# A fused LayerNorm and GELU: five-row buffers in four slots, with loads and stores on one queue

## The chip, the cores and the metric

One core of a Trainium2 chip. The time is that of one execution on the device, in microseconds (us), and lower is better. "Landing" means that one DMA engine has finished its share of a transfer and counted up the semaphore. A transfer is spread over 16 DMA engines, each with its own share of the rows, and it has landed when all 16 have counted.

## The reference

```python
x: (8, 1024, 2048) float32; gamma, beta: (2048,)
mean = np.mean(x, axis=-1, keepdims=True)
var = np.var(x, axis=-1, keepdims=True)
out = gamma * (x - mean) / np.sqrt(var + eps) + beta
return 0.5 * out * (1 + np.tanh(np.sqrt(2 / np.pi) * (out + 0.044715 * out ** 3)))
```

8192 rows of 8 KB are read once and written once: 67.1 MB in, 67.1 MB out.

## The kernel before

A buffer holds four rows for each of 128 partitions (4 MB), so a partition's share is one run of 32 KB. There are five slots and 16 buffers. SyncE issues the loads, ScalarE the stores; each has its own DMA queue. The result overwrites the input in its slot, so a slot is loaded again only when its store has landed.

```python
R = 4; SLOTS = 5; SPLIT = 3
...
@block.sync                                   # loads
for b in range(B):
    s = slot(b)
    if stored(b):
        sy.wait_ge(s_store[s], stored(b))     # the slot's last store has landed
    for q in range(R):
        if b == 0:       # four transfers of one row each
            sy.dma_start(out=xts[s][:, q:q + 1], in_=xg[0, :, q:q + 1]).then_inc(s_first[q], 16)
        elif b == SPLIT: # buffer 3 too
            sy.dma_start(out=xts[s][:, q:q + 1], in_=xg[b, :, q:q + 1]).then_inc(s_load[s], 16)
    if b not in (0, SPLIT):
        sy.dma_start(out=xts[s], in_=xg[b]).then_inc(s_load[s], 16 * R)
...
@block.vector                                 # k runs over the rows of all slots
    stats(s, q, (s_load[s], 16 * R) if q == 0 else None, k + 1)   # row t
    scale((q - 1) % R, k + 1)                                      # row t - 1
...
@block.scalar
for t in range(T + 1):
    if t < T:            # normalize row t
        ac.activation(out=yks[t % 2], in_=xts[slot(b)][:, q], func=ACT.Identity, ...)
    i = t - 1            # GELU of row t - 1, from PSUM into its slot
    ins = ac.activation(out=xt[:, q], in_=pss[i % 2], func=ACT.Gelu_apprx_tanh)._wait_ge(s_t, i + 1)
    if by_row(b):        # last buffer: a store per row
        ...
    elif q == R - 1:     # a store per buffer
        ins.then_inc(s_r, 1)
        ac.dma_start(out=og[b], in_=xt)._wait_ge(s_r, b + 1).then_inc(s_store[slot(b)], 16)
```

GpSimd computes the inverse deviation and the offset of a row, VectorE the statistics and the product with gamma, TensorE adds beta in PSUM. Mind the order on VectorE and ScalarE: the last row of a buffer is finished after the first row of the next buffer has been begun.

## Time and profile before

| | before |
|---|---|
| time | 320.19 us median (320.01 to 320.34, 4 runs) |
| span of the profiled run | 318.5 us |
| VectorE, ScalarE, TensorE busy | 78%, 79%, 77% |
| DMA, share of 16 engines | 98.4% |
| last load landed, all 16 engines | 285.0 us |

The page gives the rate in 40 equal slices and the DMA issues. The columns of an issue line are count, size, and time from issue to landing:

```profile
GB/s 289 438 457 401 394 434 430 444 424 436 432 424 444 417 453 416 440 440 416 457 403 457 420 436 444 411 461 403 453 432 424 449 407 457 424 432 403 453 396 209
...
out_dram<-xt ACTq DMA_DIRECT2D x15, 4096.0 KB, 32.6
```

Apart from the first slice (289), slice 5 (394) and the last (209) are the low ones. A store of 4 MB takes 32.6 us to land, over three times what its packets need alone (8 of 1.21 us on each engine, 9.7 us), because it shares the engines with the loads. The rest of the reading is in the prediction.

### The profile page before, as it was taken

The numbers are of one execution on the slowest core, as the hardware profiler recorded it, in microseconds if no ns is written. First come the engines' busy times: TensorE is split into PE (matmuls) and PEld (weight loads), VectorE is DVE, ScalarE is ACT, GpSimd is POOL, SyncE is SP. The second block draws the span as 40 slices with busy tenths as digits, with TensorE's granted clock in tenths as the row PEclk, the third lists the DMA queues.
The fourth block names the chain that finished last, engine by engine and source line by source line (L and its number), as shares of the span: only waits on it lengthen the run. The fifth ranks groups of instructions, "written<-read, shape, count | busy, mean of one in ns | idle before, by whom it ended". The sixth has DMA issues, their size and how long they took to land.

```text
span 318.5 us, 2090 instructions
## 1 busy us (share of the span) xinstructions
PE 244.3 (77%) x520; PEld 57.2 (18%) x520; DVE 247.5 (78%) x386; ACT 251.7 (79%) x132; POOL 110.6 (35%) x201
## 2 busy tenths in 40 slices
PE   2769999999999989687795868958589595886860
PEld 1212222222212112111121112212112121111110
DVE  3499999999999897786968968599686986869810
ACT  2769999999999989698696967969589695995970
POOL 1144444444444444232443333333332433324300
DMA  7999999999999999999999999999999999999995
GB/s 289 438 457 401 394 434 430 444 424 436 432 424 444 417 453 416 440 440 416 457 403 457 420 436 444 411 461 403 453 432 424 449 407 457 424 432 403 453 396 209
DMA packets 6002, 134.26 MB, mean 421 GB/s; under 512 B 704, under 2 KB 752, under 8 KB 752
## 3 DMA queue, kind: packets, MB, share of 16 engines
q1 hardware_dynamic: 3168, 67.11, 49.4%
q10 hardware_dynamic: 2832, 67.13, 49.0%
q14 instruction: 2, 0.02, 0.0%
HBM read 67.13 MB, written 67.11 MB: 421 GB/s over the span
## 4 chain that ended last, share of the span: by engine, by line
DMA 64%; ACT 14%; DVE 10%; POOL 5%; PE 3%; issue 1%; ACTq 0%; DVEq 0%; POOLq 0%; SPq 0%
DMA xt<-in_x_dram 32%; DMA out_dram<-xt 30%; ACT yk L195 9%; DVE sts L149 7%; ACT xt L202 4%; POOL ves L135 3%; DVE zg L158 2%; PE ps L220 2%; DMA rows<-in_gamma_dram 2%; POOL rss L137 2%; POOL nms L139 1%; DVE mvs L155 1%; PE ps L237 1%; ACT g_t L191 1%; ACTq L205 0%
## 5 line engine op out<-in xcount | busy, mean ns | idle before, releaser
L149 DVE BATCH_NORM_STATS2 sts<-xt 128x6 f32<-128x512 f32 x256 | 157.7, 679 | 33.5 <-DMA xt<-in_x_dram 31.9
L195 ACT ACTIVATE yk<-xt,nms,rss 128x2048 bf16<-128x2048 f32 x64 | 133.7, 2090 | 48.9 <-POOL nms L139 42.9
L237 PE MATMUL ps<-zg,ident 128*128 128x512 bf16 x256 | 120.8, 627 | 55.8 <-DVE zg L158 54.7
L233 PE MATMUL ps<-b_hl,ones_b 33*128 33x512 bf16 x256 | 120.6, 624 | 2.2 <-PEq L228 2.2
L202 ACT ACTIVATE xt<-ps 128x2048 f32<-128x2048 f32 x64 | 118.9, 1858 | 1.5 <-PE ps L237 1.5
L135 POOL TENSOR_SCALAR ves<-mvs 128x1 f32<-128x1 f32 x64 | 38.5, 602 | 179.2 <-DVE mvs L155 179.2
L158 DVE TENSOR_TENSOR zg<-yk,g_t 128x2048 bf16<-128x2048 bf16 x64 | 76.5, 1195 | 19.2 <-ACT yk L195 19.2
L237 PEld LDWEIGHTS ps<-zg,ident 128*128 128x128 bf16 x256 | 27.6, 130 | 149.0 <-DVE zg L158 113.7
L233 PEld LDWEIGHTS ps<-b_hl,ones_b 33*128 33x128 bf16 x256 | 27.0, 127 | 92.1 <-issue 88.4
L139 POOL TENSOR_SCALAR nms<-mvs,rss 128x1 f32<-128x1 f32 x64 | 35.7, 558 | 6.3
L137 POOL TENSOR_TENSOR rss<-ves,mhalf 128x1 f32<-128x1 f32 x64 | 35.3, 552 | 5.3
L155 DVE BATCH_NORM_AGGREGATE mvs<-sts 128x2 f32<-128x24 f32 x64 | 16.9, 264 | 2.2
L220 PE MATMUL ps<-rows,ones 1*128 1x512 f32 x8 | 7.2, 1076 | 6.1 <-DMA rows<-in_gamma_dram 6.1
L188 ACT ACTIVATE b_hl<-rows 1x2048 bf16<-1x2048 f32 x1 | 1.9, 1909 | 5.3 <-DMA rows<-in_beta_dram 5.3
L166 DVE TENSOR_TENSOR b_hl<-rows,b_hl 1x2048 bf16<-1x2048 f32 x1 | 2.3, 2280 | 2.8 <-ACT b_hl L189 2.8
L220 PEld LDWEIGHTS ps<-rows,ones 1*128 1x128 f32 x8 | 2.5, 327 | 9.2 <-DMA rows<-in_gamma_dram 6.1
L191 ACT ACTIVATE g_t<-ps 128x2048 bf16<-128x2048 f32 x1 | 1.9, 1877 | 1.9 <-PE ps L220 1.9
L184 ACT ACT_TABLE_LOAD x1 | 1.3, 1283 | 0.9 <-SPq L107 0.9
L189 ACT ACTIVATE b_hl<-rows 1x2048 bf16<-1x2048 f32 x1 | 1.9, 1908 | 0.0
L161 DVE MEMSET b_hl<- 33x1024 uint32 x1 | 0.9, 912 | 1.2 <-SPq L107 1.2
L126 POOL MEMSET ones<- 65x128 f32 x1 | 0.2, 202 | 0.5 <-SPq L107 0.5
L130 POOL TENSOR_SCALAR_AFFINE_SELECT ident<-ident 128x128 bf16<-128x128 bf16 x1 | 0.3, 295 | 0.1
(7 smaller groups left out, 0.9 us busy)
## 6 DMA issues: line engine op xcount, KB each, us to landing
out_dram<-xt ACTq DMA_DIRECT2D x15, 4096.0 KB, 32.6
xt<-in_x_dram SPq DMA_DIRECT2D x14, 4096.0 KB
xt<-in_x_dram SPq DMA_DIRECT2D x8, 1024.0 KB, 8.4
out_dram<-xt ACTq DMA_DIRECT2D x4, 1024.0 KB, 8.6
rows<-in_beta_dram ACTq DMA_DIRECT2D x2, 8.0 KB, 5.9
rows<-in_gamma_dram ACTq DMA_DIRECT2D x1, 8.0 KB, 5.1
```

The lines of the kernel that those rows point to most:

```text
L135: po.tensor_scalar(out=ves[:, c], in0=mvs[:, k, 1:2], scalar1=float(eps), scalar2=1.0, op0=ALU.add, op1=ALU.mult)._wait_ge(s_a, k + 1).the ...
L137: po.tensor_tensor(out=rss[:, c], in0=ves[:, c], in1=mhalf, op=ALU.pow)._wait_ge(s_q, 2 * k + 1).then_inc(s_q, 1)
L139: po.tensor_scalar(out=nms[:, c], in0=mvs[:, k, 0:1], scalar1=rss[:, c], scalar2=-1.0, op0=ALU.mult, op1=ALU.mult)._wait_ge(s_q, 2 * k + 2 ...
L149: ins = ve.bn_stats(out=sts[:, q, j, :], in_=xr[:, j, :])
L155: ve.bn_aggr(out=mvs[:, q], in_=sts[:, q])._wait_ge(s_o, count).then_inc(s_a, 1)
L158: ve.tensor_tensor(out=zgs[q % 2], in0=yks[q % 2], in1=g_t, op=ALU.mult)._wait_ge(s_n, count).then_inc(s_z, 1)
L191: ac.activation(out=g_t, in_=pss[0], func=ACT.Identity)._wait_ge(s_tg, 1).then_inc(s_c, 1)
L195: ac.activation(out=yks[t % 2], in_=xts[slot(b)][:, q], func=ACT.Identity, scale=rss[:, q:q + 1], bias=nms[:, q:q + 1])._wait_ge(s_p, t + ...
L202: ins = ac.activation(out=xt[:, q], in_=pss[i % 2], func=ACT.Gelu_apprx_tanh)._wait_ge(s_t, i + 1)
L220: ins = pe.matmul(pss[0][:, cols(j)], lhsT=ones[64:65], rhs=rows[64:65, j * K // nsub:(j + 1) * K // nsub, :d // K], start=True, stop=True)
L233: ins = pe.matmul(ps[:, cols(j)], lhsT=ones_b, rhs=b_hl[:, cols(j)], start=True, stop=False)
L237: ins = pe.matmul(ps[:, cols(j)], lhsT=ident, rhs=zgs[k % 2][:, cols(j)], start=False, stop=True)
```

## The change

It makes buffers larger (40 KB runs, fewer packets), puts loads and stores in a fixed order on one queue so that the last load comes early, and stores the last buffer in parts so that its computation is hidden.

```diff
-R = 4
-SLOTS = 5
-SPLIT = 3
+R = 5
+R0 = 4                      # the first buffer has four rows
+SLOTS = 4
+AHEAD = 3
+TAIL = (2, 2, 1)
...
             @block.sync
-                for b in range(B):
-                    ... loads as above
+                for b in range(SLOTS):
+                    load(b)
+                for b in range(B):
+                    s = slot(b)
+                    lo = 0
+                    for size in parts(b):
+                        stores += 1
+                        c = slice(lo, lo + size)
+                        sy.dma_start(out=og[b][:, c], in_=xts[s][:, c])._wait_ge(s_r, stores).then_inc(s_store[s], 16)
+                        lo += size
+                    if SLOTS <= b + AHEAD < B:
+                        load(b + AHEAD)          # waits for store b - 1
...
             @block.scalar
-                        ac.dma_start(out=og[b], in_=xt)._wait_ge(s_r, b + 1).then_inc(s_store[slot(b)], 16)
-                        ac.sem_inc(s_g, 1)
+                        ac.sem_inc(s_g, 1)._wait_ge(s_r, stores)
```

There are now 13 buffers. The compute instructions are the same.

More of the change, by code (lines that the diff above doesn't have):

```diff
@@ L33, with groups @@
     nsub = d // FMAX
-    assert d % FMAX == 0 and n % (P * R) == 0
+    assert d % FMAX == 0 and n % P == 0
     T = n // P
-    B = T // R
-    assert (B - 1) % SLOTS == 0
-    xg = xf.rearrange("(b p r) d -> b p r d", p=P, r=R)
-    og = of.rearrange("(b p r) d -> b p r d", p=P, r=R)
+    B = 1 + (T - R0) // R
+    assert T == R0 + R * (B - 1) and (B - 1) % SLOTS == 0 and sum(TAIL) == R and T % 4 == 0
+    n0 = P * R0
+    def groups(v):
+        return [v[:n0].rearrange("(p r) d -> p r d", p=P)] + [
+            v[n0 + b * P * R:n0 + (b + 1) * P * R].rearrange("(p r) d -> p r d", p=P) for b in range(B - 1)]
+    xg, og = groups(xf), groups(of)
     bf16 = mybir.dt.bfloat16
@@ L60 @@
     g_t = sb("g_t", [P, d], bf16)
-    sts = sb("sts", [P, R, nsub, nc.vector.BN_STATS_DIM], f32)
-    mvs = sb("mvs", [P, R, 2], f32)
-    ves = sb("ves", [P, R], f32)
-    rss = sb("rss", [P, R], f32)
-    nms = sb("nms", [P, R], f32)
+    sts = sb("sts", [P, 4, nsub, nc.vector.BN_STATS_DIM], f32)
+    mvs = sb("mvs", [P, 4, 2], f32)
+    ves = sb("ves", [P, 4], f32)
+    rss = sb("rss", [P, 4], f32)
+    nms = sb("nms", [P, 4], f32)
     def sem(name):
         return tc.alloc_semaphore(name)
-    s_first = [sem(f"first{q}") for q in range(R)]
+    s_first = [sem(f"first{q}") for q in range(R0)]
     s_load = [sem(f"load{s}") for s in range(SLOTS)]
@@ L99, in cols, with parts, place @@
         return slice(j * FMAX, (j + 1) * FMAX)
-    def by_row(b):
-        return b == B - 1
+    def parts(b):
+        return TAIL if b == B - 1 else (R if b else R0,)
     def stored(b):
-        return sum(16 * (R if by_row(c) else 1) for c in range(b) if slot(c) == slot(b))
+        return sum(16 * len(parts(c)) for c in range(b) if slot(c) == slot(b))
+    def place(t):
+        return divmod(t, R0) if t < R0 else (1 + (t - R0) // R, (t - R0) % R)
     with tc.tile_critical(no_gpsimd_drain=True):
@@ L111, in _, with load @@
             def _(sy):
-                for b in range(B):
+                stores = 0
+                def load(b):
                     s = slot(b)
@@ L115, in _ @@
                         sy.wait_ge(s_store[s], stored(b))
-                    for q in range(R):
-                        if b == 0:
-                            sy.dma_start(out=xts[s][:, q:q + 1], in_=xg[0, :, q:q + 1]).then_inc(s_first[q], 16)
-                        elif b == SPLIT:
-                            sy.dma_start(out=xts[s][:, q:q + 1], in_=xg[b, :, q:q + 1]).then_inc(s_load[s], 16)
-                    if b not in (0, SPLIT):
-                        sy.dma_start(out=xts[s], in_=xg[b]).then_inc(s_load[s], 16 * R)
+                    if b == 0:
+                        for q in range(R0):
+                            sy.dma_start(out=xts[s][:, q:q + 1], in_=xg[0][:, q:q + 1]).then_inc(s_first[q], 16)
+                    else:
+                        sy.dma_start(out=xts[s], in_=xg[b]).then_inc(s_load[s], 16)
+                for b in range(SLOTS):
[10 more added lines that the diff above has]
+                        load(b + AHEAD)
             @block.gpsimd
@@ L131, in _ @@
                                  pattern=[[-1, P]], channel_multiplier=1)._wait_ge(s_setp, 1).then_inc(s_setp, 1)
-                with po.Fori(0, B):
-                    for k in range(R):
+                with po.Fori(0, T // 4):
+                    for k in range(4):
                         c = slice(k, k + 1)
@@ L140, in _, with stats @@
                                          op0=ALU.mult, op1=ALU.mult)._wait_ge(s_q, 2 * k + 2).then_inc(s_p, 1)
-                    po.sem_inc(s_a, -R)
-                    po.sem_inc(s_q, -2 * R)
+                    po.sem_inc(s_a, -4)
+                    po.sem_inc(s_q, -8)
             @block.vector
             def _(ve):
-                def stats(s, q, wait, count):
+                def stats(s, q, m, wait, count):
                     xr = xts[s][:, q].rearrange("p (s f) -> p s f", f=FMAX)
                     for j in range(nsub):
-                        ins = ve.bn_stats(out=sts[:, q, j, :], in_=xr[:, j, :])
+                        ins = ve.bn_stats(out=sts[:, m, j, :], in_=xr[:, j, :])
                         if j == 0 and wait:
@@ L152, in stats, with scale @@
                             if wait[0] is s_load[s]:
-                                ins.then_inc(s_load[s], -16 * R)
+                                ins.then_inc(s_load[s], -16)
                     ins.then_inc(s_o, 1)
-                    ve.bn_aggr(out=mvs[:, q], in_=sts[:, q])._wait_ge(s_o, count).then_inc(s_a, 1)
-                def scale(q, count):
-                    ve.tensor_tensor(out=zgs[q % 2], in0=yks[q % 2], in1=g_t,
+                    ve.bn_aggr(out=mvs[:, m], in_=sts[:, m])._wait_ge(s_o, count).then_inc(s_a, 1)
+                def scale(t, count):
+                    ve.tensor_tensor(out=zgs[t % 2], in0=yks[t % 2], in1=g_t,
                                      op=ALU.mult)._wait_ge(s_n, count).then_inc(s_z, 1)
                 ve.memset(b_hl, 0.0).then_inc(s_m, 1)
-                for q in range(R):
-                    stats(slot(0), q, (s_first[q], 16), q + 1)
+                for q in range(R0):
+                    stats(slot(0), q, q, (s_first[q], 16), q + 1)
                     if q == 0:
@@ L170, in _ @@
                         scale(q - 1, q)
-                ve.sem_inc(s_o, -R)
-                ve.sem_inc(s_n, -(R - 1))
+                ve.sem_inc(s_o, -R0)
+                ve.sem_inc(s_n, -(R0 - 1))
                 with ve.Fori(0, (B - 1) // SLOTS):
@@ L175, in _ @@
                         s, q = divmod(k, R)
-                        stats(s, q, (s_load[s], 16 * R) if q == 0 else None, k + 1)
-                        scale((q - 1) % R, k + 1)
+                        stats(s, q, k % 4, (s_load[s], 16) if q == 0 else None, k + 1)
+                        scale(k - 1, k + 1)
                     ve.sem_inc(s_o, -SLOTS * R)
                     ve.sem_inc(s_n, -SLOTS * R)
-                scale(R - 1, 1)
+                scale(T - 1, 1)
             @block.scalar
@@ L191, in _ @@
                 ac.activation(out=g_t, in_=pss[0], func=ACT.Identity)._wait_ge(s_tg, 1).then_inc(s_c, 1)
+                stores = 0
                 for t in range(T + 1):
                     if t < T:
-                        b, q = divmod(t, R)
-                        ac.activation(out=yks[t % 2], in_=xts[slot(b)][:, q], func=ACT.Identity, scale=rss[:, q:q + 1],
-                                      bias=nms[:, q:q + 1])._wait_ge(s_p, t + 1).then_inc(s_n, 1)
+                        b, q = place(t)
+                        ac.activation(out=yks[t % 2], in_=xts[slot(b)][:, q], func=ACT.Identity,
+                                      scale=rss[:, t % 4:t % 4 + 1], bias=nms[:, t % 4:t % 4 + 1])._wait_ge(
+                                          s_p, t + 1).then_inc(s_n, 1)
                     i = t - 1
@@ L199, in _ @@
                         continue
-                    b, q = divmod(i, R)
-                    xt = xts[slot(b)]
-                    ins = ac.activation(out=xt[:, q], in_=pss[i % 2], func=ACT.Gelu_apprx_tanh)._wait_ge(s_t, i + 1)
-                    if by_row(b):
-                        ins.then_inc(s_r, 1)
-                        ac.dma_start(out=og[b, :, q:q + 1], in_=xt[:, q:q + 1])._wait_ge(
-                            s_r, b + q + 1).then_inc(s_store[slot(b)], 16)
-                        ac.sem_inc(s_g, 1)
-                    elif q == R - 1:
-                        ins.then_inc(s_r, 1)
-                        ac.dma_start(out=og[b], in_=xt)._wait_ge(s_r, b + 1).then_inc(s_store[slot(b)], 16)
-                        ac.sem_inc(s_g, 1)
+                    b, q = place(i)
+                    ins = ac.activation(out=xts[slot(b)][:, q], in_=pss[i % 2],
+                                        func=ACT.Gelu_apprx_tanh)._wait_ge(s_t, i + 1)
+                    if q + 1 in [sum(parts(b)[:k + 1]) for k in range(len(parts(b)))]:
+                        stores += 1
+                        ins.then_inc(s_r, 1)
+                        ac.sem_inc(s_g, 1)._wait_ge(s_r, stores)
                     else:
@@ L228, in _ @@
                 pe.sem_inc(s_g, 2)
-                with pe.Fori(0, B):
-                    for k in range(R):
+                with pe.Fori(0, T // 4):
+                    for k in range(4):
                         ps = pss[k % 2]
@@ L241, in _ @@
                         ins.then_inc(s_t, 1)
-                    pe.sem_inc(s_g, -R)
-                    pe.sem_inc(s_z, -R)
+                    pe.sem_inc(s_g, -4)
+                    pe.sem_inc(s_z, -4)
         for b in range(B, B + SLOTS):
```

## The prediction

> **What bounds the kernel now.** I began with the page: busy shares, the slices in time, the queues.
>
> ```profile
> PE 244.3 (77%) x520; PEld 57.2 (18%) x520; DVE 247.5 (78%) x386; ACT 251.7 (79%) x132; POOL 110.6 (35%) x201
> ...
> DMA  7999999999999999999999999999999999999995
> ...
> DMA packets 6002, 134.26 MB, mean 421 GB/s; under 512 B 704, under 2 KB 752, under 8 KB 752
> ...
> q1 hardware_dynamic: 3168, 67.11, 49.4%
> q10 hardware_dynamic: 2832, 67.13, 49.0%
> ```
>
> No compute engine is above 79%, while the DMA row is at 9 in every slice but the first and the last. q1 carries the loads (SyncE) and q10 the stores (ScalarE): 49.4 + 49.0 = 98.4% of 16 engines' time. The input has to be read once and the output written once, so the bytes are fixed. What is left to win is 1.6% of 318.5 us of idle time (5 us), the dead time inside packets, and any difference between mixed and one-way traffic.
>
> Next I read the chain that ended last and SyncE's waits.
>
> ```profile
> DMA 64%; ACT 14%; DVE 10%; POOL 5%; PE 3%; issue 1%; ACTq 0%; DVEq 0%; POOLq 0%; SPq 0%
> ```
>
> ```profile
> SPq L122 <- DMA out_dram<-xt: 240.3, 11, 47.2
> ```
>
> ```profile
> 215.78 35.01 DMA out_dram<-xt
> 250.80 34.20 DMA xt<-in_x_dram
> ```
>
> The chain is a store (35 us), then the load that waited for its slot (34 us), then a few rows of compute, and so on. A 4 MB transfer would take about 9.7 us at full rate. It takes 34 to 35 because loads and stores share the engines and queue behind each other. The chain says "slot", but the slots only pass on the limit of the DMA engines. Shortening the way through one slot moves the end only if it fills a gap in DMA.
>
> Third, the windows: their last two columns are the DMA share of 16 engines and GB/s.
>
> ```profile
> 38.00:42.00 4.00, 3.27 (x8) 0.70 (x7) 3.46 (x6) 4.00 (x3) 1.63 (x3) 1.00 1.04 365
> 50.00:280.00 230.00, 185.13 (x401) 42.70 (x400) 190.67 (x301) 191.00 (x101) 86.26 (x150) 1.00 1.00 433
> 286.00:304.00 18.00, 12.97 (x29) 3.04 (x30) 14.52 (x23) 13.37 (x8) 6.54 (x12) 1.00 0.99 424
> ```
>
> From 50 to 280 us, with loads and stores mixed, the engines move 433 GB/s without a gap. From 38 to 42 us they are busy (1.04) but slow (365): there the load of the fourth buffer runs, which is split into four transfers with 8 KB packets. (A window credits a packet to its start, so short ones are off by a few per cent.) From 286 us on only stores are left.
>
> The records of single packets give the rest. A 32 KB packet takes 1213 ns (median), load or store. An 8 KB one takes 309. The 512 packets of the split load average 336: (336.4 - 309) x 512 / 16 = 0.88 us per engine. The landings of single engines show one more thing: 15 of 16 engines finish the last load by 283.8 us and the last store by 315.4, one finishes at 285.0 and 317.0. One engine trails by 1.2 to 1.7 us and sets the end. It starts at 1.9 us and has no gap.
>
> **What the Trainium skill says.** "DMA: Bandwidth & Descriptors", section Specifications, gives a fabric ceiling of 435 GB/s for the 16 engines; the trace has 433 in the mixed stage, so the rate itself has nothing left. The same page, section "Issuing engines are not separate DMA queues", says that transfers issued by different engines run on the same 16 DMA engines and that issuing from several only saves issue time. The trace fits: a DMA issue on ScalarE takes 0.34 us, 19 of them, on an engine that isn't the limit. Section "Queues, rings and completion order" says that each engine works through a ring in order and that the semaphore's write is held until earlier writes of that engine have landed. Whether that stalls the next transfer in the same ring decides a rival below. In the trace it doesn't for transfers of one direction: the single-row stores at the end follow each other every 2.5 us on an engine (312.1, 314.6, 317.0 on the trailing one), which is eight packets of 309 ns and nothing more.
>
> **The change, part by part.**
>
> 1. Runs of 40 KB. From the two medians, 8 KB of data cost (1213 - 309) / 3 = 301.3 ns and each packet has 7.7 ns on top. Packets per engine before: loads 64 of 8 KB and 112 of 32 KB, stores 32 and 120, 328 in all. After: loads 32 of 8 KB and 96 of 40 KB; stores 8 of 32 KB, 88 of 40 KB, 16 of 16 KB, 8 of 8 KB, 248 in all. The saving is 80 x 7.7 ns = 0.6 us. There are also 34 transfers where there were 44, so 10 fewer semaphore writes per engine at 9 ns, 0.1 us.
>
> 2. The split load goes. It was there so that 8 KB loads would let the first store pass in the round robin of two queues. With one queue its 0.9 us excess disappears, if that excess comes from the 8 KB packets.
>
> 3. One queue. Order in each ring: load b+2, store b, load b+3, store b+1. No transfer needs to arrive early, only before its turn. Let load b+2 begin at 0 and a 5-row transfer take 8 x 1.514 = 12.1 us. Load b+3's turn is 24.2; it needs store b-1 landed, which is at about 1. Store b's turn is 12.1; its data came in at -36.3, and five rows take some 29 us from first statistics to last GELU (25.2 for the four rows of the last buffer, 285.1 to 310.3, plus 4.1 more), so it is ready at about -7. Slack is 19 us or more, so I expect no gap. The tightest place is the start: the first four row loads have landed by 13.7 us, so their data ends near 13.2; three loads of 12.1 us end near 49.5, and store 0 takes 8 x 1.213 = 9.7 more, to 59.2. Store 1 needs nine rows. The timeline issues stores every 16.4 us, 4.1 per row, with the first at 36.0, so it is ready at 36.0 + 5 x 4.1 = 56.5. It fits by 2.7 us.
>
> 4. The tail. Today the last load lands at 285.0 and then two stores of 4 MB remain. After, three stores of 5 MB (36 us) remain behind the last load, and its five rows need 29. The last parts (2, 2, 1 rows) are ready at about +17.5, +26.2 and +29.5 and have their turn at +24.3, +29.2 and +34.1. The trailing engine had no gap in the tail before either, so hiding the computation of the last buffer wins nothing.
>
> 5. ScalarE loses its DMA issues, 19 x 0.34 = 6.5 us, off the path. The added waits on SyncE cost nothing there. Compute instructions are the same.
>
> Sum: 0.6 + 0.1 + 0.9 = 1.6 us, of which I take 1.4: 320.14 - 1.4 = 318.7 us.
>
> **Rivals.** (a) A change of direction within one ring costs something, for instance because the last writes of a store hold up the loads behind. There are about 24 changes; 0.1 us each would give 321.1, 0.5 us 331. For it: two queues can fill such a stall from the other, one can't. Against it: store after store shows none, and in the mixed stage the engines alternate directions packet by packet at 433 GB/s. (b) SyncE, now in strict order, holds back a load behind a store whose rows aren't ready. A late first or last store would cost 1 to 3 us: 320 to 322. For: the 2.7 us margin at the start. Against: the slack everywhere else. (c) The trailing engine loses less. Its lag grows with the stores, whose packets on it are 15 to 25 ns longer; if that is per packet, 40 KB runs save another 0.4 us, and if it comes from mixing directions up to 1.5 us: 317. Against: its store packets are as slow after 286 us, with no loads left. (d) The 0.9 us of the split load returns elsewhere, because it belonged to the first store's start: 319.6.
>
> **Range and chances.** 2% is 6.4 us, more than all idle time in the DMA row, and the bytes are fixed: faster 0.02. Slower by 2% needs a stall of a third of a microsecond or more at each change of direction, or a mistake of mine in the order: 0.04. The range of 317.2 to 321.2 holds (b), (c), (d) and a light form of (a).
>
> **What would show it.** Right: one data queue near 98 to 99%, in the steady stage 433 to 435 GB/s, packets of 40 KB at about 1514 ns, packets some 4,560 instead of 6,002, no slow stretch near 40 us, and the row of slices at 9 through the tail. In the chain, waits for loads would still stand, as DMA stays the limit. Wrong: gaps in the DMA row at changes of direction (rival a), a fall near 60 us (rival b), or 40 KB runs cut into smaller packets. A time below 316 would say that mixed traffic in two queues costs something that I don't see.

## The result, and the profile after

321.93 us median (321.23 to 322.16, 4 runs) against 320.19. The ratio is 1.0051, 95% interval 1.0036 to 1.0066. A ratio here is the mean of one kernel's fast runs over the mean of the other's of the same rounds, so it isn't quite the ratio of the medians. Executions over 1.5% slower than the fastest of the same kernel are left out of the means. The change is slower by half a per cent: outside the predicted range of 317.2 to 321.2, and against its direction. The profiled run is the fastest of the four (321.23).

The page of the changed kernel:

```profile
span 319.4 us, 2073 instructions
...
DMA  7999998999999999999999999999999999998995
...
DMA packets 4562, 134.26 MB, mean 420 GB/s; under 512 B 544, under 2 KB 592, under 8 KB 592
...
q1 hardware_dynamic: 4464, 134.22, 98.1%
```

4562 packets, as worked out, and all of the data on one queue. 98.1% of 319.4 us and, before, 98.4% of 318.5 us are both some 313.4 us per engine, though 80 fewer packets should have saved 0.6 us. So the packets have become longer by about what was saved, and the rest of the loss is idle time of the engines that don't end last (about 5 us before, 6 after).

Its chain, and what SyncE waited for:

```profile
DMA 53%; DVE 17%; ACT 13%; POOL 9%; PE 3%; issue 2%; SPq 0%; POOLq 0%; DVEq 0%; ACTq 0%
```

```profile
SPq L142 <- ACT xt L226: 276.0, 15, 31.1
SPq L132 <- DMA out_dram<-xt: 21.5, 7, 4.3
```

```profile
217.44 27.85 DMA out_dram<-xt
...
245.31 36.26 DMA xt<-in_x_dram
```

SyncE now waits for computed rows (276 us) and hardly for landed stores (21.5, where it was 240.3). The chain still alternates between a store and a load that waited for it, and it ends in the rows of the last buffer. The last load has landed by 281.6 us, 3.4 us sooner than before: the order did what it was made for.

The windows show where the rate falls. The last two columns are the DMA share and GB/s:

```profile
46.00:50.00 4.00, 3.28 (x9) 0.71 (x7) 3.48 (x6) 4.00 (x3) 1.61 (x3) 1.00 0.87 281
60.00:280.00 220.00, 176.14 (x381) 40.70 (x382) 179.85 (x283) 181.58 (x96) 84.92 (x144) 1.00 1.00 431
```

From 46 to 50 us, where the first store follows the last of the first loads, the rate falls to 281. From 60 to 280 us it is 431 (it was 433 from 50 to 280). The page averages over 16 engines and hides the rest, so I went to the records of single packets and landings. A 40 KB packet takes 1514 ns (median), but some take up to 2768. Three columns sum this up for all runs; "stretched" is what packets took beyond the usual time of their size, where that is over 30 ns, divided by 16 engines. "Lag" is the landing of the last engine behind the middle one, near 290 us.

| run | time, us | stretched after 60 us | lag, us |
|---|---|---|---|
| before | 320.2 | 0.14 | 2.4 |
| after | 321.9 | 0.90 | 3.3 |
| c: before, no split load | 320.0 | 0.07 | 2.5 |
| b: before, one queue | 322.9 | 0.80 | 5.9 |
| a: after, two queues | 322.8 | 0.61 | 3.4 |
| d1: after, halves in order | 322.9 | 0.71 | 4.3 |
| d2: after, halves interleaved | 322.2 | 0.52 | 3.8 |
| h2: after, pieces of 4 packets | 322.4 | 1.64 | 4.5 |
| f1: copy, one queue | 321.4 | 1.08 | 4.5 |
| f2: copy, two queues | 317.6 | 0.00 | 0.3 to 2.2, not growing |
| f3: copy, loads then stores | 318.6 | 0.06 | 0.1 |

In the changed kernel the long packets stand where a load ends and a store is queued behind it in the same ring. I call this a turn; by the code the changed kernel has ten from load to store. On the engine that ends last, the last packet of the load is longer by 1.25 us at the first turn (48 us), and by 0.18, 0.48, 0.07, 0.33, 0.27, 0.24 and 0.06 us at 83, 108, 132, 157, 180, 228 and 253 us: 1.6 us in all after the first. (The records don't name the engine; I followed it by which packet starts where another ends.) Its lag grows from 1.3 to 3.3 us and sets the end.

### The profile page after: what moved, and what is told of

The parts are those of the page before. It is cut to its first block, busy times and chain, and to the rows that moved or that the text cites. A ratio compares the mean times of both kernels' runs of the same rounds, so it can differ in the third digit from the quotient of the medians.

```text
span 319.4 us, 2073 instructions
## 1 busy us (share of the span) xinstructions
PE 244.3 (76%) x520; PEld 57.2 (18%) x520; DVE 248.1 (78%) x386; ACT 252.1 (79%) x132; POOL 114.5 (36%) x201
## 2 busy tenths in 40 slices
DMA packets 4562, 134.26 MB, mean 420 GB/s; under 512 B 544, under 2 KB 592, under 8 KB 592
## 3 DMA queue, kind: packets, MB, share of 16 engines
q1 hardware_dynamic: 4464, 134.22, 98.1%
## 4 chain that ended last, share of the span: by engine, by line
DMA 53%; DVE 17%; ACT 13%; POOL 9%; PE 3%; issue 2%; SPq 0%; POOLq 0%; DVEq 0%; ACTq 0%
DMA xt<-in_x_dram 35%; DMA out_dram<-xt 17%; DVE sts L172 11%; ACT yk L219 10%; POOL ves L158 5%; DVE zg L181 4%; POOL rss L160 3%; PE ps L240 2%; ACT xt L226 2%; DMA rows<-in_gamma_dram 2%; POOL nms L162 1%; DVE mvs L178 1%; PE ps L257 1%; ACT g_t L214 1%; SPq L142 0%
## 5 line engine op out<-in xcount | busy, mean ns | idle before, releaser
L158 POOL TENSOR_SCALAR ves<-mvs 128x1 f32<-128x1 f32 x64 | 45.0, 702 | 176.4 <-DVE mvs L178 176.4
L162 POOL TENSOR_SCALAR nms<-mvs,rss 128x1 f32<-128x1 f32 x64 | 33.4, 521 | 6.3
```

The source lines that it names most:

```text
L158: po.tensor_scalar(out=ves[:, c], in0=mvs[:, k, 1:2], scalar1=float(eps), scalar2=1.0, op0=ALU.add, op1=ALU.mult)._wait_ge(s_a, k + 1).the ...
L162: po.tensor_scalar(out=nms[:, c], in0=mvs[:, k, 0:1], scalar1=rss[:, c], scalar2=-1.0, op0=ALU.mult, op1=ALU.mult)._wait_ge(s_q, 2 * k + 2 ...
```

## The experiments

In the order of the questions. Three rounds or five with the kernel before on the same chip, unless said otherwise.

### Which part of the change costs: a and b

Edit of a: the changed kernel, stores back on ScalarE.

```diff
 @block.sync
-    sy.dma_start(out=og[b][:, c], in_=xts[s][:, c])._wait_ge(s_r, stores).then_inc(s_store[s], 16)
 @block.scalar
-    ac.sem_inc(s_g, 1)._wait_ge(s_r, stores)
+    ac.dma_start(out=og[b][:, c], in_=xts[slot(b)][:, c])._wait_ge(s_r, stores).then_inc(s_store[slot(b)], 16)
+    ac.sem_inc(s_g, 1)
```

> The changed kernel with its stores issued by ScalarE again, so loads and stores have a queue each; five rows, four slots and the tail of 2, 2, 1 stay. Theory 1 (in one ring the last packets of a load are lengthened where a store follows, and this adds up on the trailing engine): the lengthened packets after 60 us go, 319 to 320 us, at most 320.5. Theory 2 (the five-row buffers, four slots or 40 KB packets cost the time, whatever the queue): it stays at 321.5 to 322.3 us.

Edit of b: the kernel before, its stores on SyncE, load b+4 behind store b.

```diff
 @block.sync
+    for b in range(SLOTS): load(b)
+    for b in range(B):
+        sy.dma_start(out=og[b], in_=xts[s])._wait_ge(s_r, b + 1).then_inc(s_store[s], 16)   # last buffer: per row
+        if SLOTS <= b + SLOTS - 1 < B: load(b + SLOTS - 1)
 @block.scalar
-    ac.dma_start(out=og[b], in_=xt)._wait_ge(s_r, b + 1).then_inc(s_store[slot(b)], 16)
```

> The kernel before (four rows, five slots, split load, single-row tail) with its stores on SyncE's queue, load b+4 behind store b. It has 15 turns from load to store in place of the changed kernel's 12 or so. Theory 1: slower than before, 321.5 to 323 us, with lengthened last packets of loads and a growing lag of one or two engines. Theory 2: 319.7 to 320.5 us, as before.

a: 322.81 us (321.54 to 324.54), ratio 1.0082 (1.0058 to 1.0105). b: 322.89 us (322.54 to 323.24), ratio 1.0082 (1.0069 to 1.0095). So each part alone is slower than before; b is also slower than both together, while the intervals of a and the changed kernel overlap. a lies above the ranges of both theories. In b one engine lags by 5.9 us, though eight of the 16 have landed the last row by 314.4 and 15 by 317.6; the last lands at 319.9. That is as the theory of the turn has it. (By the code b has 12 turns from load to store and the changed kernel 10, not 15 and 12 as the expectation says.) a contradicts the theory as I had put it, for it has two queues and is slow. Its windows and its chain tell why:

```profile
291.00:294.00 3.00, 2.28 (x6) 0.57 (x5) 2.44 (x5) 2.86 (x2) 1.61 (x3) 1.00 0.03 14
```

```profile
292.10 1.77 ACT xt L219
293.87 0.02 issue
293.89 0.34 ACTq L226
```

From 291 to 294 us all DMA engines are idle (0.03, 14 GB/s). Store 11 is issued at 293.89, right after the GELU of its last row. On ScalarE that GELU comes after the first row of buffer 12, and load 12 landed at 285.0. So the last store but one waits for the last load. The last experiments take that up.

The trace of a shows a second thing that the theory doesn't foresee. Packets are stretched with two queues too (0.61 us after 60 us), and the lag at the landings of loads grows from 0.4 us at 37 us to 4.1 at the last one: the middle engine has finished load 12 at 280.9 us, the last at 285.0. In a3, below, it is the same (0.82 us, and a lag of 4.2). So a second queue alone doesn't stop the lag from growing. In f2 (below), a copy on two queues without computation, it doesn't grow; what makes the difference isn't tested.

### Where the slow stretch near 40 us belongs: c and g1

Edit of c, in the kernel before:

```diff
-SPLIT = 3
+SPLIT = -1
```

> The kernel before with buffer 3 loaded by one transfer of 4 MB rather than four of 1 MB. My prediction's second step (the 0.9 us of slow packets near 40 us belong to the 8 KB packets): 319.0 to 319.5 us and no slow stretch near 40 us. Rival d of the prediction (they belong to the first store's start): 320 us or more, with 32 KB load packets lengthened near 40 us.

319.97 us (319.94 to 320.04), ratio 0.9995 (0.9982 to 1.0008).

```profile
38.00:42.00 4.00, 3.27 (x8) 0.70 (x7) 3.46 (x6) 4.00 (x3) 1.62 (x3) 1.00 0.86 303
```

The slow stretch is still there (303 GB/s; it was 365 with the split load). Packets are stretched by 0.84 us per engine between 10 and 60 us, against 0.79 with the split. So the 0.9 us don't come from the 8 KB packets, and rival d of the prediction holds.

g1 adds to c a small store in the first microseconds:

```diff
+    ac.dma_start(out=og[0, :, 0, 0:128], in_=warm)._wait_ge(s_wset, 1).then_inc(s_warm, 16)
```

> The kernel before without the split load, plus one store of 512 B per row into the first buffer's output in the first microseconds, overwritten later by the right rows. If the 0.8 us of stretched load packets near 38 us belong to the first store that the program makes: they go, 319.0 to 319.4 us. If they belong to the first meeting of a full load and a store: they stay, 319.9 to 320.3 us.

320.28 us (320.09 to 320.56), ratio 1.0006 (0.9993 to 1.002), and 0.81 us of stretched packets as before. It isn't that a program's first store is dear. What it is, these runs leave open; it happens where the first full store comes up against full loads.

### Is it DMA alone: f1, f3 and f2

Three copies: no computation, the loaded rows are stored as they are, in the changed kernel's sizes and slots. Their outputs are wrong, which doesn't matter for the times. f1 keeps its order on one queue; f2 gives the stores to ScalarE's queue; f3 makes all loads and then all stores.

```python
# f1
for b in range(SLOTS): load(sy, b)
for b in range(B):
    sy.wait_ge(s_load[slot(b)], upto(b)); store(sy, b)
    if SLOTS <= b + AHEAD < B:
        sy.wait_ge(s_store[slot(b - 1)], upto(b - 1)); load(sy, b + AHEAD)
```

> Wrong on purpose: no computation, the loaded rows are stored as they are, with the changed kernel's transfers in the changed kernel's order on one queue. Theory 1 and 3: the lengthened load packets and the growing lag are all there, as they come from DMA alone: 320 to 322 us. Rival: they come from the compute engines' use of the buffers or from late issues: then about 317 us and a lag that stays under 2 us.

> Wrong on purpose: all loads, then all stores, on one queue, same sizes and bytes, one turn only. If turns cost: 316 to 317.5 us, lengthened packets only at the start and near the one turn, and the lag of the last store is what the trailing engine's stores bring by themselves (about 1.5 us). If the lag comes with the stores and not with the turns: the same lag and time as the copy with 12 turns.

> Wrong on purpose: the copy with stores on ScalarE's queue and loads on SyncE's, same sizes and slots. Theory 3 (lag grows where load packets end among other engines' stores): mixed all along, so a lag of 2 to 3 us and 319 to 320 us, less than the 321.4 us of the copy on one queue. If the queue doesn't matter: 321 us or more.

f1: 321.37 us (320.82 to 321.91). f3: 318.62 (318.53 to 318.89), above its range. f2: 317.57 (317.3 to 317.63), below its range, against theory 3. Queues and rates of f1:

```profile
q1 hardware_dynamic: 3744, 134.22, 97.9%
```

```profile
60.00:280.00 220.00, 0.00 (x0) 1.00 1.00 431
```

and of f2:

```profile
q1 hardware_dynamic: 1872, 67.11, 49.7%
q10 hardware_dynamic: 1872, 67.11, 49.1%
```

```profile
60.00:280.00 220.00, 0.00 (x0) 1.00 1.00 432
```

The same bytes in the same packets differ by 3.8 us (1.1% by the two ratios to the kernel before, 1.0031 and 0.9918), with no compute engine in play. (With its second queue f2 also drops the fixed order of loads and stores; these runs don't tell the two apart.) The mean rates hardly differ (431 and 432), which is why the averaged views show so little: the cost falls on few engines. The middle one has landed the last store at 313.9 us in f1 and 313.8 in f2, the last one at 318.5 and 314.5. In f1 the lag is 0.2 us at 72 us, and it grows at the landings of loads (0.8 at 108, 1.3 at 132, 2.0 at 157, 2.9 at 181, 4.1 at 229) and not at those of stores. In f2 no packet is stretched after 60 us, and its lag is 0.3 us at the landings of loads and 2.1 to 2.2 at those of stores, all the way from 33 to 283 us. In f3 hardly any is beyond the start (0.06 us), and the lag is 0.1 us through all stores, so stores alone make no lag either. The rate of f3 in slices:

```profile
GB/s 318 448 424 413 449 444 429 413 434 460 424 418 418 470 429 418 413 465 434 341 397 463 413 413 413 465 444 413 413 413 496 413 413 413 491 418 413 413 418 325
```

Only slice 20 (341) is low: there the ring runs empty at its one turn, for some 1.3 us (158.5 to 159.8), and no packet is stretched.

### Is it the queued store behind the load: f4 and f5

f1 with one wait more, one look each, state unknown. In f4 a store is issued only when the load ahead of it has landed; in f5 a load only when the store ahead of it has.

```diff
 # f4, before store(sy, b)
+    sy.wait_ge(s_load[slot(last)], upto(last))
 # f5, before load(sy, b + AHEAD)
+    sy.wait_ge(s_store[slot(b)], upto(b))
```

> Wrong on purpose: the copy on one queue, but each store is issued only when the load ahead of it in the ring has landed, so no store is queued behind a load. Some 12 gaps of about 1.5 us: about 336 us. Read the packets, not the time. If load packets are stretched because stores follow or run on other engines while they end: none is stretched after the start, and the lag stays near 0.6 us. If any end of a load stretches packets: as in the copy without the waits.

> Wrong on purpose: the mirror of it, each load is issued only when the store ahead of it has landed; stores are still queued behind loads. About as long. If it is the turn from load to store that stretches: stretched load packets as in the plain copy, though the lag is set back at each gap.

f4 took 340.1 us, f5 357.42. The rows of f5's slices show the gaps:

```profile
DMA  8999999979979979988988997996998997999996
```

In f4 the packets at the ends of loads are normal (0.04 us at 86 and 112 us), as expected. But some 0.8 us per engine now stand at the ends of stores (packets that start near 71, 97 and 125 us), with loads queued behind them. In f5 the ends of loads, with stores queued behind, are stretched by some 1.1 to 1.4 us on all 16 engines (84, 112, 142 us), far more than at the later turns of f1 (0.05 to 0.23 us per engine, on a few of them), and the first packets of loads that start on an empty ring by some 0.6 (at 73 and 101 us), much as at the start of the program. So in these two copies the end of a transfer is stretched where the other direction is queued behind it, and not where the ring was drained first. I had expected it only for stores behind loads; f4 shows it for loads behind stores, where f1 shows hardly any at the same places. Why some turns stretch and others don't isn't settled by this.

### Number of turns or length of phases: d1, d2, h2, h1, h3

d1 and d2 cut loads and stores of the changed kernel into parts of 3 and 2 rows. In d1 the order is store, store, load, load; in d2 store, load, store, load.

```diff
+    steps = [("store", halves[0]), ("load", halves[0]), ("store", halves[1]), ("load", halves[1])]
+    if not INTERLEAVE:
+        steps = [steps[0], steps[2], steps[1], steps[3]]
```

> Changed kernel, loads and most stores cut into parts of 3 and 2 rows, in the order store, store, load, load: more packets (24 and 16 KB), as many turns from load to store as before the edit. It is the control of the next run. About 7.7 ns for each of some 170 more packets per engine, 1.3 us: 322.5 to 324 us by every theory.

> The same packets, in the order store part, load part, store part, load part: nearly twice the turns in the one ring. Theory 1 (each turn from load to store costs the trailing engine 0.2 to 0.3 us): 2 to 3 us over the control. Theory 3 (what costs is that an engine out of step still loads while the others store; shorter phases against the same lag mean loads and stores are mixed more of the time, as in two queues): no slower than the control, and less lag.

d1: 322.93 us (322.41 to 323.05), ratio 1.0084. d2: 322.2 (321.89 to 322.62), ratio 1.0064. Nearly twice the turns cost nothing; if anything d2 is a little faster. That goes against a fixed price for each turn.

h2, h1 and h3 keep the packets of 40 KB and interleave store and load in 2, 4 or 8 pieces of the partitions:

```diff
+    for i in range(CUT):                        # CUT = 2, 4, 8
+        c = slice(i, P, CUT)
+        sy.dma_start(out=og[b][c], in_=xts[s][c])...
+        sy.dma_start(out=xts[slot(n)][c], in_=xg[n][c])...
```

> Store and load interleaved in 2 pieces each, every second partition: phases of 4 packets of 40 KB per engine in place of 8, turns doubled, packets as in the changed kernel. If the length of a one-way phase matters and not the count of turns: 320.3 to 321.3 us (the interleaved halves without their 1.3 us of extra packets). If each turn costs: 323 us or more.

> The same in 4 pieces, 2 packets per engine in a phase. Phase length: 319 to 320.5 us, no stretched packets after the first turn. Turns: 325 us or more. If pieces of 32 spread partitions cost bandwidth by themselves, packets of loads and stores are longer throughout, and the run says nothing on either.

> The same in 8 pieces, one packet per engine in a phase, so loads and stores alternate packet by packet in one ring, much as two queues do. Phase length: as two queues in the plain copy, 318.5 to 320 us, less about 7 x 2 x 12 more semaphore writes of 9 ns, 1.5 us at most. Turns: 330 us or more.

h2: 322.37 us (321.64 to 322.43), between the two expectations. h1: 323.97 us in its one fast run; three more at 331.0 to 331.7 count as slow. h3: 411.09 us (407.1 to 412.85, 417.44 in a slow one), ratio 1.27. Its steady stage:

```profile
60.00:280.00 220.00, 127.68 (x277) 29.55 (x276) 132.01 (x208) 132.00 (x70) 61.85 (x105) 1.00 0.98 302
```

302 GB/s with the engines busy (0.98): a 40 KB packet takes 1983 ns in the mean, 1731 in the median. My guess that shorter phases in one ring would behave like two queues was wrong, and by a lot: two rings alternate at 433 GB/s (the kernel before). From 8 to 4 packets a phase little if anything is lost (ratios of 1.0051 and 1.0058), at 1 packet 89 us are. But h1 and h3 don't separate turns from something else that they change: their pieces take every fourth or eighth partition, where a whole transfer takes them all. A cost of that isn't excluded, nor is one of issues, which take SyncE 0.6 to 0.7 us apiece (median) in h3. What is shown is that this way of mixing in one ring is no remedy.

### Why two queues with five-row buffers were slow: a2, c2, a3, c3

a2 is a, c2 is c, with the last row of a buffer finished before the next buffer's first row is begun.

```diff
 @block.vector
+    if q == 0: scale(k - 1, k + 1)
     stats(s, q, ...)
+    if q != 0: scale(k - 1, k + 1)
 @block.scalar: likewise, GELU of row t - 1 ahead of the first row of a buffer
```

> The two-queue variant of the changed kernel, with the last row of a buffer finished (scale on VectorE, GELU on ScalarE) before the first row of the next buffer is begun. If the hold made the gap of some 4.7 us in the DMA at 290 us: store 11 is issued some 3 us earlier and the time falls by 1 to 3 us, to 320 to 321.8; the five rows after the last load still end late. If the gap has another cause: 322.8 us as before.

> The kernel before without the split load and with the same new order. Its trailing DMA engine has no gap in the tail, so by the theory that this engine sets the end nothing changes: 319.7 to 320.3 us. If earlier stores keep both queues fuller and hold the lag down, up to 1.5 us less: 318.5 to 319.5.

333.09 us and 337.75 us, ratios 1.040 and 1.055. The experiment failed: the new order drains the pipeline at every buffer. In a2 stores are then issued every 24.1 us, about what the DMA needs for five rows in and out (2 x 12.1), so compute can never make up for its late start, and store 11 is issued at 300.35. The runs say nothing on the held store. They do show how little room compute has: at 4.1 us a row it needs 20.5 of the 24.2 us.

a3 and c3 do it only where the next buffer is in the last slot, so at buffers 4, 8, 12 (a3) and 5, 10, 15 (c3).

```diff
-    if q == 0: scale(k - 1, k + 1)
+    if (s, q) == (SLOTS - 1, 0): scale(k - 1, k + 1)
```

> The two-queue variant of the changed kernel, the last row of a buffer finished before the next buffer's first row only where the next buffer is in slot 3 (buffers 4, 8 and 12). If store 11 was held by the last load: it is issued at 290 to 291 us in place of 293.9, the gap in DMA near 290 us shrinks from 4.7 to about 1.5 us, and the time is 320.3 to 322 us. If not: 322.8 us and the same gap.

> The kernel before without the split load, with the same order for buffers 5, 10 and 15 only. The trailing DMA engine has no gap in the tail there, so 319.7 to 320.3 us; the small gap of the other engines near 294 us goes.

a3: 321.8 us (321.35 to 322.1), ratio 1.0041 (1.0025 to 1.0056). Store 11 is issued at 289.37, and the idle stretch is filled:

```profile
291.00:294.00 3.00, 0.76 (x2) 0.28 (x3) 2.04 (x3) 2.83 (x2) 0.88 (x3) 1.00 1.02 437
```

So the gap of a was the held store, worth about 1 us of its time. What is left in a3 is the tail: its last stores are issued at 310.0 and 313.4 us, when their rows are ready, and all 16 engines land together near 318.7. Five rows after a last load near 285 end too late.

c3: 319.84 us (319.73 to 319.92), ratio 0.9985 (0.9971 to 0.9998). It is the fastest correct kernel here, by 0.15%, which is hardly worth a line in the source. The two-queue kernels c and c3 are the best, and neither beats the kernel before by much.

## Why the prediction was right or wrong

**What bounds the kernel:** right. It is the DMA engines, and of these the one that trails. In the changed kernel it sets the end again: all but one land the last row by 317.6 us, the last at 317.9, most at 316.2.

**Step 1 (fewer, larger packets):** right. 4562 packets as said, 40 KB in 1514 ns as said. Its 0.7 us don't show by themselves. d1, with some 170 packets more per engine, took 1.0 us more than the changed kernel, where the price of 7.7 ns gives 1.3, so the size is plausible.

**Step 2 (the split load):** wrong. The 0.9 us weren't the 8 KB packets' but belong to the meeting of the first full store with loads (c, f1). I had named this as rival d and given it too little weight: the window from 38 to 42 us couldn't tell the two apart, as both happen there. On the trailing engine the first turn even became dearer in the profiled runs: 1.25 us on one packet, where the stretched packets of the kernel before near 39 us add up to some 0.5 on its trailing engine.

**Step 3 (one queue):** the order was right, its conclusion wrong. No ring runs dry at the start: store 1 was issued at 56.7 us (I had 56.5) and store 0 landed at 61.4. But a ring without gaps was taken for one without cost. The inference that failed stands in rival a: "in the mixed stage the engines alternate directions packet by packet at 433 GB/s". That was seen with two rings, and I carried it over to one. The plain copies show it: two rings 317.57 us and no stretched packet after 60 us, one ring 321.37. The other argument, that store follows store without a stall, was right but doesn't bear on a turn. Rival a was right in kind: one ring with 10 turns from load to store (19 changes of direction, where I had counted about 24) took 3.8 us more than two rings in the plain copy, some 0.4 us for each such turn if spread evenly. They aren't even, and doubling their number costs nothing (d2, h2), so the sum "turns times a price" that I wrote for it isn't the right form. Nor would the sign that I gave for it, gaps in the DMA row, have shown it: only two slices of the row fall, to 8, at the first turn and near 291 us, and the loss that decides is a lag of few engines.

**Step 4 (the tail):** right in its times. The parts were issued 17.3, 25.7 and 29.1 us after the last load landed at 281.56, where I had 17.5, 26.2 and 29.5. I overlooked that store 11 is held until the last load has landed: it was issued at 290.45, 8.9 us after it, so most engines had a gap near 291 us. The trailing engine had none: stores 10 and 11 land on it 12.1 us apart, which is the bare transfer. So this didn't move the end.

**Step 5 (ScalarE's issues):** right, as far as the runs show. f1 has the loss with no work on ScalarE at all.

**The sum.** I expected 1.4 us less and got 1.7 more, 3.1 us apart; in the profiled run, 321.23, it is 2.5. On the trailing engine of that run the later turns account for 1.6, and the first turn, where I had booked a gain of 0.9 and it lost 0.8 against before, for 1.7 more. That is 0.8 more than needed. The kernel before has many slightly longer store packets on its trailing engine (15 to 25 ns each), and the changed one has fewer, which goes the right way, but I can't place it packet by packet.

**Why the parts don't add up.** Five-row buffers on two queues end 2.6 us later than before: the last load lands late, as one engine lags by 4.1 us, and the tail behind it is too long (a, a3). One queue with four-row buffers ends 2.6 us later, as one engine lags by 5.9 us (b). Together 1.7: the one-queue order lands the last load at 281.6 rather than 285.0 us and hides the tail, and the five-row buffers end with a lag of 3.3 us rather than 5.9. That they lag less because they have fewer turns (10 against 12) is possible, but only argued.

**Left open:** what in the hardware stretches a packet at a turn, why f1 is spared at the ends of stores and f4 isn't, why one engine falls behind more than the others, and why the lag grows in a and a3, which have two queues, and not in f2.

## What to carry to other kernels

Where the DMA engines are full, don't put loads and stores in one queue unmeasured: here that cost 3.8 us of 321 in the plain copy and 2.6 us in the kernel with four-row buffers (b). A second queue is no cure by itself: with five-row buffers and computation, two queues (a, a3) were not clearly faster than one. If a kernel is bound by DMA, look at the landing of each engine and at single packets, not only at mean shares: a loss on one of 16 engines hardly shows in the mean and still sets the end. And when a fact is seen in one arrangement, such as free mixing of directions in two rings, measure it in the new one before counting on it.

## What the Trainium skill lacked or had wrong

- "DMA: Bandwidth & Descriptors", section "Issuing engines are not separate DMA queues", says that issuing from several engines only saves issue time. Here a second queue saved 3.8 us of 321.4 in a copy (f1 and f2) that has only 26 transfers and keeps the engines full meanwhile (share 1.00 in both); the last engine, not the issues, makes the difference. In the kernel with five-row buffers it saved nothing clear (a).
- "Perfetto Trace Analysis", section "DMA Optimizations", advises one engine for inputs and another for outputs "to allow more dynamic spread". The advice agrees with f2 against f1, less with a. It lacks what was measured here: packets at a turn in one ring can take longer, by 0.05 to 0.23 us per engine at the later turns of f1 and 1.1 to 1.4 us in f5.
- No page that I read tells of a first meeting of full loads and stores that stretches packets by 0.5 to 1.1 us per engine (b, c, f1, f2), whatever the queue.
- "DMA: Bandwidth & Descriptors", section "Latency and other measured facts", says that DMA engines 7 and 15 are usually slower in traces, guesses at a cause that belongs to GpSimd's queue alone, and gives no size. Here everything runs on the sync and scalar queues, and one engine (the records don't say which) lagged by 2.4 us in the kernel before, 5.9 us in b, and 0.1 us at the stores of f3, where loads and stores don't meet.
